# Eighteen weight differences of a decoder layer, on GpSimd in place of VectorE

## The chip, the cores and the metric

The kernel runs on one core of a Trainium2 chip. The time is device time in microseconds (us) of one execution, the median of the runs. A core has four engines that compute here: TensorE (PE in the profile) multiplies matrices, VectorE (DVE) and ScalarE (ACT) work elementwise, and GpSimd (POOL) is a fourth, programmable engine that this kernel uses mainly to issue some DMAs. SyncE (SP) issues most of the other DMAs. Each engine works through its own queue in order; engines wait for each other and for DMAs through semaphores.

## The reference

One decoder layer on 256 tokens of width 2048, in float32. Cut to what matters:

```
h    = rms_norm(x, pre_norm_w)
proj = h @ w_in                         # all projections and gates at once
oa   = gated_delta_rule(conv(q), conv(k), conv(v), beta, g)   # branch A, 8 heads
u_a  = (norm(oa) * silu(z_a)) @ w_branch_a        # 1024 -> 2048
ob   = block_attention(q, k, v) * silu(z_b)       # branch B, 8 heads
u_b  = ob @ w_branch_b                            # 1024 -> 2048
y    = (sigmoid(ga) * u_a + sigmoid(gb) * u_b) @ w_out        # 2048 -> 2048
out  = x + rms_norm(y, post_norm_w)
```

## The kernel before

Every large product is made from halves: a float32 tile is cast to a shorter form (`hi`, on ACT, line 218) and the rest is taken as a second tile (`lo = raw - hi`, on DVE, line 219), and TensorE multiplies hi by hi, hi by lo and lo by hi. Weights stream from HBM in blocks of 128 x 4 x 512 numbers (1 MB); each block is split in two sets of 128 x 1024. The pool that holds the `hi` and `lo` tiles has three buffers of each, so ACT and DVE can be up to three sets ahead of TensorE. Both inputs of the `lo` subtraction lie in SBUF.

Some of the matrix products are replaced by a scheme of the Strassen kind: a product of 2 x 2 blocks is made with seven block products in place of eight (`seven`). It needs four sums of the left side's blocks and four of the weight's. The weight's quarters that enter the sums are loaded unsplit (`fetch`, line 726, DMAs issued by GpSimd) into three tiles `tq[0]`, `tq[1]`, `tq[2]`; `differences` (lines 728 to 735) then forms, in place, `tq[0] - tq[2]`, `tq[1] - tq[0]` and `tq[1] - tq[2]`, each in two instructions of 128 x 1024 numbers: six a group. A fourth difference is formed later by DVE inside `seven` (line 786). The three groups are the two column pairs of `w_branch_a` (products named `ua0p` and `ua2p`) and one part of `w_out` (`yp`). In the profile the first group's tiles are called `tq_g` and `tq_z`, those of the others `tq`. All the groups reuse buffers: the second and third lie in the same three (`z0`, `z1`, `z2`), one of which the first uses as well, so a group is fetched as tiles of the one before come free.

The first product that reads a difference is `p5`, the second of the seven; `p6` and `p7` follow. As in any other product, each difference is split by ACT and DVE before TensorE multiplies with it.

What sets the order: TensorE's instructions keep the order in which the program traces them (`pin`, that is `keep_in_program_order`, which ties an instruction behind the one traced before it on its engine). Side work sits in queues of generators (`Queue`); after every few matmuls `tick()` advances them, and a `yield` of some number waits that many ticks' worth. The differences are one such generator, in queue `sq`, which waits `T_WAIT` (5, 7, 7) and then hands out one instruction per unit. The six are pinned on DVE in the kernel before. What is not pinned, such as the splits and the DMAs, is put in order on its engine by the planner that builds the program, by when it takes the inputs to be ready.

Beside the differences of the first group runs the end of the attention branch (scores of a head at lines 1010 to 1016, the keys' scaling at line 1055) and the projections `ga`, beside the second the gate `gb` (`raw_gb`, `lo_gb`), beside the third the last of `gb` and the projection `ub`.

Of the kernel before, what the change touches and what calls it, by code (L numbers as in the profile page):

```python
# [12 lines left out]
ALU = mybir.AluOpType  # L13
# [61 lines left out]
def hybrid_layer(  # L75
# [15 lines left out]
    nc = tc.nc  # L91
# [49 lines left out]
    pin = tc.keep_in_program_order  # L141
# [586 lines left out]
    def differences(tq, c, wait):  # L728
        yield wait
        for o, a, b in ((0, 0, 2), (1, 1, 0), (2, 1, 2)):  # L730
            for u in range(2):
                us = slice(2 * u, 2 * u + 2)
                pin(nc.vector.tensor_tensor(tq[o][:, us], tq[a][:, us], tq[b][:, us], op=ALU.subtract))
                yield 1
        formed.append(c)

# [97 lines left out]
    def next_differences(w, c):  # L834


        for q in aq + bq:
            q.drain()
        tqs.append([big.tile([P, 4, 512], F32, tag=f"z{i}", name=f"tq{len(tqs)}_{i}") for i in range(3)])
        for i in (2, 0, 1) if len(tqs) == 2 else (1, 0, 2):  # L840
            fetch(tqs[-1], w, c, i)
        formed.clear()
        sq.add(differences(tqs[-1], c, T_WAIT[len(tqs) - 1]))

    def solve():
# [136 lines left out]
        for i in (0, 2, 1):  # L982
            fetch(tqs[0], wa, 0, i)
        sq.add(differences(tqs[0], 0, T_WAIT[0]))
        yield OS_WAIT
        while attended[0] < H:
# [290 lines left out]
```

## Time and profile before

| | |
|---|---|
| median of 3 runs | 782.95 us (782.21 to 784.22) |
| the profiled execution | 782.22 us |
| its span, first to last instruction | 780.4 us |
| mean granted TensorE clock | 0.998 |
| differences on DVE | 18, from 439.1 to 645.0 us |

A row of a timeline reads: start, duration (us), engine, line, operation, output <- inputs by the program's names, shapes, count, and in brackets how long the engine was idle before it and what ended that. A row of waits reads: who waited for whom, us in total, times, the longest. A row of a grouped view gives the count, then busy time and the mean ns of one. PEld is TensorE's loading of weights, which lies beside its multiplications. Busy TensorE is not TensorE at its peak; spans on POOL are rough.

### The profile page before, as it was taken

Reading aid. Unit: us, or ns where it says so; the run is one execution under the profiler, and the core shown is the slowest. Engines: PE = TensorE matmul, PEld = TensorE weight load, DVE = VectorE, ACT = ScalarE, POOL = GpSimd, SP = SyncE. Lnnn points to the kernel's source line nnn. Section 1 sums busy time; section 2 is a strip of 40 time slices with the busy share of each in tenths; the row PEclk is TensorE's granted clock in tenths of the full one; section 3 lists DMA queues with packets and bytes.
Section 4 is the critical chain, followed back from the end, with each engine's and each line's share of the span. In section 5 each row is a group of like instructions: output and inputs, shape, how many; then the busy total and the mean of one; then the engine's idle time right before and its main releaser. Section 6 shows DMA issues by size and latency. Waiting matters only on the chain.

```text
span 780.4 us, 10345 instructions
## 1 busy us (share of the span) xinstructions
PE 765.1 (98%) x3923; PEld 651.2 (83%) x3923; DVE 564.1 (72%) x914; ACT 424.7 (54%) x642; POOL 31.5 (4%) x57
## 2 busy tenths in 40 slices
PE   8999999998999999999999999999999999999996
PEld 7898988897888888888888888878887788887884
DVE  5777669885867899775546785685748677878753
ACT  5676665655545544554447574654456544556641
POOL 3000001111000000002001000000000000000000
PEclk9999999999999999999999999999999999999999
DMA  8576675468865657659434557557563965475822
GB/s 300 173 235 214 188 211 169 135 185 205 244 207 167 211 165 214 174 161 244 123 109 166 212 165 249 206 202 247 176 212 129 356 215 169 155 259 187 312 106 108
DMA packets 93656, 153.44 MB, mean 197 GB/s; under 512 B 3237, under 2 KB 46886, under 8 KB 92966
## 3 DMA queue, kind: packets, MB, share of 16 engines
q1 hardware_dynamic: 88902, 134.42, 53.4%
q0 software_dynamic: 3936, 15.21, 5.5%
q10 hardware_dynamic: 768, 3.15, 1.6%
q8 instruction: 31, 0.51, 0.3%
q14 instruction: 19, 0.16, 0.1%
HBM read 149.61 MB, written 3.15 MB: 196 GB/s over the span
## 4 chain that ended last, share of the span: by engine, by line
PE 91%; DVE 3%; ACT 3%; DMA 2%; issue 1%; SPq 0%; DVEq 0%; ACTq 0%
PE a_gb L144 11%; PE a_ga L144 11%; PE a_y L144 10%; PE a_zg L144 6%; PE a_mk L144 6%; PE a_k L144 6%; PE a_ub L144 6%; PE a_zm L144 6%; PE a_mq L144 5%; PE a_mv L144 5%; PE a_v L144 5%; PE a_q L144 4%; PE a_ua L144 3%; PE sv L144 2%; PE s L144 1%
## 5 line engine op out<-in xcount | busy, mean ns | idle before, releaser
L144 PE MATMUL a_ga<-hi_ga,hT 128*128 128x512 f32 x256 | 82.2, 393 | 0.0
L144 PE MATMUL a_gb<-hi_gb,hT 128*128 128x512 f32 x256 | 79.9, 390 | 0.0
L219 DVE TENSOR_TENSOR lo_gb<-raw_gb,hi_gb 128x1024 fp32r<-128x1024 f32 x32 | 38.7, 1224 | 25.9 <-ACT hi_gb L218 25.7
L144 PEld LDWEIGHTS a_gb<-hi_gb,hT 128*128 128x128 f32 x256 | 48.1, 188 | 10.0
L144 PEld LDWEIGHTS a_ga<-hi_ga,hT 128*128 128x128 f32 x256 | 48.1, 188 | 9.8
L219 DVE TENSOR_TENSOR lo_ga<-raw_ga,hi_ga 128x1024 fp32r<-128x1024 f32 x32 | 38.8, 1221 | 17.9 <-ACT hi_ga L218 17.8
L144 PE MATMUL a_gb<-lo_gb,hT 128*128 128x512 f32 x128 | 50.4, 394 | 0.6 <-DVE lo_gb L219 0.4
L144 PE MATMUL a_ga<-lo_ga,hT 128*128 128x512 f32 x128 | 50.1, 391 | 0.7 <-DVE lo_ga L219 0.7
L218 ACT CAST hi_gb<-raw_gb 128x1024 fp32r<-128x1024 f32 x32 | 33.3, 1052 | 31.9 <-PE a_gb L144 24.4
L218 ACT CAST hi_ga<-raw_ga 128x1024 fp32r<-128x1024 f32 x32 | 33.5, 1052 | 30.9 <-PE a_ga L144 16.7
L144 PE MATMUL a_zg<-hi_zg,hT 128*128 128x348 f32 (+1 forms) x192 | 47.0, 322 | 0.0
L144 PE MATMUL a_v<-hT,hi_v 128*128 128x512 f32 x128 | 45.4, 398 | 1.4 <-ACT hi_v L218 1.4
L144 PE MATMUL a_mq<-hT,hi_mq 128*128 128x512 f32 x128 | 46.7, 405 | 0.0
L144 PE MATMUL a_mk<-hT,hi_mk 128*128 128x512 f32 x128 | 46.0, 401 | 0.0
L144 PE MATMUL a_y<-hi_y,mT 128*128 128x512 f32 x144 | 45.9, 391 | 0.0
L144 PE MATMUL a_q<-hT,hi_q 128*128 128x512 f32 x128 | 45.8, 398 | 0.0
L144 PE MATMUL a_ub<-hi_ub,obT 128*128 128x512 f32 x128 | 41.0, 393 | 0.0
L144 PE MATMUL a_k<-hT,hi_k 128*128 128x512 f32 x128 | 40.6, 400 | 0.0
L144 PE MATMUL a_zm<-hi_zm,hT 128*128 128x512 f32 x128 | 40.6, 392 | 0.0
L144 PE MATMUL a_mv<-hi_mv,hT 128*128 128x512 f32 x128 | 40.1, 391 | 0.0
L144 PE MATMUL a_v<-hT,lo_v 128*128 128x256 f32 x128 | 36.1, 282 | 1.4 <-DVE lo_v L219 1.4
L144 PE MATMUL a_q<-hT,lo_q 128*128 128x256 f32 x128 | 35.9, 280 | 0.0
(375 smaller groups left out, 1962.4 us busy)
## 6 DMA issues: line engine op xcount, KB each, us to landing
raw_ga<-in_w_in_dram SPq DMA_DIRECT2D x16, 1024.0 KB, 5.3
raw_gb<-in_w_in_dram SPq DMA_DIRECT2D x16, 1024.0 KB, 5.2
raw_y<-in_w_out_dram SPq DMA_DIRECT2D x15, 1024.0 KB, 5.3
raw_q<-in_w_in_dram SPq DMA_DIRECT2D x8, 1024.0 KB, 5.7
raw_mv<-in_w_in_dram SPq DMA_DIRECT2D x8, 1024.0 KB, 5.0
raw_v<-in_w_in_dram SPq DMA_DIRECT2D x8, 1024.0 KB, 10.7
raw_zm<-in_w_in_dram SPq DMA_DIRECT2D x8, 1024.0 KB, 5.1
raw_mq<-in_w_in_dram SPq DMA_DIRECT2D x8, 1024.0 KB, 5.9
```

The costliest lines, as they stand in the source:

```text
L144: return pin(nc.tensor.matmul(*args, **kwargs))
L218: nc.scalar.copy(hi, raw)
L219: nc.vector.tensor_tensor(lo, raw, hi.bitcast(F32), op=ALU.subtract)
```

## The change

The six subtractions of each group are issued on GpSimd in place of VectorE, and without `pin`. The tiles, the ticks and the fetches stay as they are, and so does the fourth difference in `seven`.

```
@@ differences(tq, c, wait) @@
         for o, a, b in ((0, 0, 2), (1, 1, 0), (2, 1, 2)):
             for u in range(2):
                 us = slice(2 * u, 2 * u + 2)
-                pin(nc.vector.tensor_tensor(tq[o][:, us], tq[a][:, us], tq[b][:, us], op=ALU.subtract))
+                nc.gpsimd.tensor_tensor(tq[o][:, us], tq[a][:, us], tq[b][:, us], op=ALU.subtract)
                 yield 1
```

More of the change, by code (lines that the diff above doesn't have):

```diff
@@ L732, in differences @@
                 us = slice(2 * u, 2 * u + 2)
-                pin(nc.vector.tensor_tensor(tq[o][:, us], tq[a][:, us], tq[b][:, us], op=ALU.subtract))
+                nc.gpsimd.tensor_tensor(tq[o][:, us], tq[a][:, us], tq[b][:, us], op=ALU.subtract)
                 yield 1
```

## The prediction

> **What bounds the kernel now.** I read the page first, then the list of TensorE's waits, then the three stretches in which the 18 differences run, and in those the order of single instructions. The profiled execution took 782.22 us, 780.4 of it the span; the median of the three timed runs, 782.95, is 0.7 above it, so 0.7 is added to a sum at the end. A change under 0.3% of it (2.35 us) counts as none: the runs themselves lie 2.0 us apart.
>
> ```profile
> span 780.4 us, 10345 instructions
> PE 765.1 (98%) x3923; PEld 651.2 (83%) x3923; DVE 564.1 (72%) x914; ACT 424.7 (54%) x642; POOL 31.5 (4%) x57
> PE 91%; DVE 3%; ACT 3%; DMA 2%; issue 1%; SPq 0%; DVEq 0%; ACTq 0%
> ```
>
> TensorE (PE) is busy 98% of the span and 91% of the chain that ended last. VectorE (DVE) has 72%, GpSimd (POOL) 4%. So time goes only where PE is made to wait, and what is to be asked of a change on DVE and POOL is whether PE waits more or less. The waits of PE on DVE behind the first differences, and on the outputs just ahead of them:
>
> ```profile
> PE a_ga L144 <- DVE lo_ga L219: 0.7, 2, 0.4
> PE pt L147 <- DVE oz L913: 0.5, 1, 0.5
> PE a_gb L144 <- DVE lo_gb L219: 0.4, 1, 0.4
> PE a_y L144 <- DVE lo_y L219: 0.4, 1, 0.4
> ```
>
> They make 2.0 us. In the stretches that hold the differences (stretch, length, busy time of PE, PEld, DVE, ACT and POOL, granted clock, DMA) there are none:
>
> ```profile
> 436.00:464.00 28.00, 28.00 (x145) 23.66 (x144) 24.67 (x37) 18.10 (x31) 0.00 (x0) 1.00 0.50 169
> 536.00:566.00 30.00, 30.00 (x134) 24.86 (x133) 20.28 (x18) 12.86 (x13) 0.00 (x0) 1.00 0.61 205
> 625.00:650.00 25.00, 25.00 (x112) 20.71 (x111) 18.27 (x16) 10.75 (x11) 0.00 (x0) 1.00 0.60 207
> ```
>
> PE is busy in all of 28, 30 and 25 us at a clock of 1.00, and POOL does nothing.
>
> **What is removed.** Six differences for each of the three groups:
>
> ```profile
> L733 DVE TENSOR_TENSOR tq<-tq,tq x12: 1217/1218/1220, 545.1 to 645.0; 128x1024 f32<-128x1024 f32 x12
> L733 DVE TENSOR_TENSOR tq_g<-tq_g x2: 1216/1216/1217, 439.1 to 443.0; 128x1024 f32<-128x1024 f32 x2
> L733 DVE TENSOR_TENSOR tq_z<-tq_z,tq_g x2: 1207/1212/1217, 446.5 to 448.9; 128x1024 f32<-128x1024 f32 x2
> L733 DVE TENSOR_TENSOR tq_g<-tq_z,tq_g x2: 1215/1216/1216, 456.6 to 460.3; 128x1024 f32<-128x1024 f32 x2
> ```
>
> 18 x 1.22 = 21.9 us of DVE time go. PE waits for DVE nowhere in these stretches, so this is worth nothing to the end: a gain of 0.
>
> **When POOL starts.** On POOL a difference waits only for its quarters to land and for POOL's own queue; the ticks at which it is handed out no longer delay it, and nothing keeps it in place. POOL's rows (issue of the loads), and issue to landing of four of them:
>
> ```profile
> 421.50 1.53 POOL L726 DMA_DIRECT2D tq_g<-in_w_branch_a_dram  x2 [61.08 <-ACT jo L898]
> 427.52 0.75 POOL L726 DMA_DIRECT2D tq_z<-in_w_branch_a_dram  x1 [4.50 <-DVE oz L913]
> 528.84 0.75 POOL L726 DMA_DIRECT2D tq<-in_w_branch_a_dram  x1 [36.23 <-DVE lo_ua0p L219]
> 615.01 0.75 POOL L726 DMA_DIRECT2D tq<-in_w_out_dram  x1 [11.33 <-DVE lo_ua2p L219]
> ```
> ```profile
> tq_g<-in_w_branch_a_dram POOLq DMA_DIRECT2D x1, 1024.0 KB, 8.4
> tq_z<-in_w_branch_a_dram POOLq DMA_DIRECT2D x1, 1024.0 KB, 8.9
> tq<-in_w_branch_a_dram POOLq DMA_DIRECT2D x1, 1024.0 KB, 5.6
> tq<-in_w_out_dram POOLq DMA_DIRECT2D x1, 1024.0 KB, 6.4
> ```
>
> The second load of the first row was issued at 421.50 + 0.77 = 422.3 and landed 8.4 later. So the first two differences can start at 430.7, the next four at 427.52 + 8.9 = 436.4; the second group's six at 528.84 + 5.6 = 534.4, the third's at 615.01 + 6.4 = 621.4. No load of POOL is queued behind a group but the next group's, which needs the same buffers empty, and the two at the end of the kernel, at 695.8 and later: moving the differences into POOL's queue delays no transfer.
>
> **When they must be done.** The first ACT cast that reads a group, per group:
>
> ```profile
> 508.62 1.05 ACT L218 CAST hi_ua0p<-tq_g 128x1024 fp32r<-128x1024 f32 x1 [1.67 <-PE a_ga L144]
> L218 ACT CAST hi_ua2p<-tq x8: 1048/1055/1057, 578.3 to 612.4; 128x1024 fp32r<-128x1024 f32 x8
> L218 ACT CAST hi_yp<-tq x8: 1047/1055/1057, 694.7 to 725.2; 128x1024 fp32r<-128x1024 f32 x8
> ```
>
> (For the first group this is its third set, formed last.) From 436.4 to 508.6, 534.4 to 578.3 and 621.4 to 694.7 there are 72, 44 and 73 us. The cover runs out only where one POOL difference takes over 18 us in the first group (four of them after 436.4) or 22 in the second (the two that its first product reads). As a latency the change costs 0.
>
> **What a POOL difference takes.** No row shows this form on POOL. The nearest rows of POOL:
>
> ```profile
> L623 POOL TENSOR_SCALAR_AFFINE_SELECT tv<-tv 32x1024 f32<-32x1024 f32 x4 | 4.6, 1141 | 0.3
> L621 POOL MEMSET tv<- 128x1024 f32 x1 | 0.9, 942 | 0.0
> ```
>
> One input of the same length in and out takes 1.14 us, writing alone 0.94. With all streams side by side a difference takes 1.14; with its two inputs one behind the other 2.28; with the write behind both 3.22. I take the middle, since the select's 1.14, which holds a read and a write, is near the 0.94 of the write alone, so that the write hides and only the second read adds. The Trainium skill (GPSIMD Engine Reference, Performance versus the Vector engine) gives 4.497 us for twice this length, an estimate of 2.25, by which the sum below would be 0.5 lower; no row here shows it.
>
> **What it does to DVE.** This is the unknown that decides. Six differences back to back are some 14 us in which POOL reads and writes SBUF while DVE goes on making `lo` halves out of two SBUF tiles. The trace has no moment at which both do so, so the cost is bounded: at 0, if they run side by side, and, if one holds the other up for the length of an instruction, by the following count. The rows of the second group:
>
> ```profile
> 535.82 1.23 DVE L219 TENSOR_TENSOR lo_gb<-raw_gb,hi_gb 128x1024 fp32r<-128x1024 f32 x1 [1.12 <-ACT hi_gb L218]
> 538.54 1.22 DVE L219 TENSOR_TENSOR lo_gb<-raw_gb,hi_gb 128x1024 fp32r<-128x1024 f32 x1 [1.49 <-ACT hi_gb L218]
> ```
> ```profile
> 537.46 1.05 ACT L218 CAST hi_gb<-raw_gb 128x1024 fp32r<-128x1024 f32 x1 [1.67 <-PE a_gb L144]
> ```
> ```profile
> 542.92 0.39 PE L144 MATMUL a_gb<-lo_gb,hT 128*128 128x512 f32 x1
> ```
>
> A `lo` every 2.72 us. There are three buffers, and the cast of 537.46 waited for PE to free one, so PE is two sets of 2.72 us away from the `lo` that ends at 538.54 + 1.22 = 539.76: its first use is the row at 542.92, a slack of 3.15 us. If POOL and DVE take turns, one turn is 2.28 + 1.22 = 3.50, and each `lo` falls 0.78 further behind its 2.72. DVE had been idle 1.12 before the row of 535.82, so it is free at 534.7 and lets POOL in; POOL holds until 537.0, the next `lo` ends at 538.2 instead of 537.05, late by 1.17. With five more turns the sixth is late by 1.17 + 5 x 0.78 = 5.1, and PE stands 5.1 - 3.15 = **1.9 us**. The third group has the same beat, with POOL in at 621.4:
>
> ```profile
> 621.98 1.22 DVE L219 TENSOR_TENSOR lo_gb<-raw_gb,hi_gb 128x1024 fp32r<-128x1024 f32 x1 [1.10 <-ACT hi_gb L218]
> ```
>
> First lateness 621.4 + 2.28 - 621.98 = 1.7, the sixth 5.6, less 3.15: **2.5 us**. In the first group other work stands in DVE's queue:
>
> ```profile
> 440.24 0.42 DVE L1055 TENSOR_TENSOR y_mk<-y_mk,rrow 128x256 f32<-128x256 f32 x1
> 447.73 1.21 DVE L219 TENSOR_TENSOR lo_ga<-raw_ga,hi_ga 128x1024 fp32r<-128x1024 f32 x1
> ```
> ```profile
> 449.42 0.39 PE L144 MATMUL a_ga<-lo_ga,hT 128*128 128x512 f32 x1
> ```
>
> From 430.7, six differences (13.7), the four `lo` between them (4.9) and two multiplies of the key rows like this one (0.8) end at 450.1. The `lo` of 447.73 is then done at 451.3 where PE wants it at 449.42: **1.9 us**. What is queued behind a held `lo` is all of DVE's work; here the attention's maxima and reciprocals, which fit beside POOL's last two.
>
> The sum by turns is 1.9 + 2.5 + 1.9 = 6.3 us: 782.2 + 6.3 = 788.5 as profiled, **789.2** as a median. With 1.14 for a difference a turn is 2.36, under 2.72, and nothing is lost; at 2.05 the same count gives 2.1 us, just inside what counts as none. With 3.22 a turn is 4.44: 1.72 per `lo`, so 2.1 + 8.6 - 3.15 = 7.6, 2.6 + 8.6 - 3.15 = 8.1, and 1.9 + 6 x 0.94 = 7.5 us, 23.2 in all, 806.1. I take turns over side by side as a judgement: no row speaks against either, but there is no row from which a gain could come.
>
> The Trainium skill (SBUF — State Buffer, Who interferes with whom, and the section on SBUF's two sides) says that GpSimd's one port pair is VectorE's second one, held exclusively for a whole instruction against a VectorE instruction with two SBUF inputs. By it the turns hold, and the sum is 789.2; without it, 783. No run so far shows it.
>
> **The rivals.**
> - *Side by side.* POOL's reads leave DVE's `lo` at 1.22 us, or stretch it to no more than 2.72, which the beat hides. For it: DVE is idle 1.49 before the `lo` of 538.54. Against it: nothing measured. Time 783.0, within 0.3%. Chance 0.24.
> - *POOL keeps its place* for all six. Then a `lo` asked for at 535.8 ends at 534.7 + 13.7 + 1.2 = 549.6, late by 12.6, and PE stands 9.4 per group: some 28 us, 811. For it: POOL's next difference is always ready. Against it: DVE's `lo` is waiting at each change. Chance 0.07.
> - *Faster.* In the first stretch DVE is busy 24.67 of 28 us and has the `lo` of 447.73 only 0.5 us ahead of its use; without the differences it runs up to 3.7 us earlier. It would decide if this took away PE's waits on DVE; those are 2.0 us in all, none in the stretch, so even all of them give 780.9, and a faster kernel needs order changes elsewhere too. Chance 0.05.
> - *The differences come late*, or POOL's unpinned order puts a load behind them. PE would stand at the second product of a group. It takes 18 us per difference: 0.02, with over 800.
>
> **How the numbers follow.** Turns have the remaining 0.62, of which 0.10 lies at differences so short (under 2.05 us) that less than 2.35 us is lost. Their own range is 784 to 800. Side by side has too much to leave out, so the range starts at 781.8 and ends at 800, leaving POOL's holding on, the 3.22 end and the faster case outside. Slower: 0.52 + 0.07 + 0.02, and 0.02 of side by side with a `lo` stretched past its beat = 0.63. Within: 0.10 + 0.22 = 0.32. Faster 0.05.
>
> **What would show it.** Right: `lo` rows of about 2 to 3.5 us (or as long a gap before them) at 431 to 450, 535 to 556 and 622 to 643, and PE waits on `lo` there of 1 to 3 us each, while the 18 POOL rows end long before 508, 578 and 694. Wrong: `lo` at 1.22 throughout and PE still busy all through these stretches; or POOL rows far from 2.3 us, which move the sum by the count above; or a difference on POOL that PE waits for.

## The result

The changed kernel takes 793.0 us (median; 792.45 to 794.31) against 783.5 for the kernel before on the same chip: 1.0125 times as long, 95% interval 1.0111 to 1.0140, or 9.5 us more. The forecast was slower, 789.2 us, in a range of 781.8 to 800. The changed kernel's profiled execution took 794.31 us, 12.1 more than that of before; 1.7 of these lie ahead of the first difference, where nothing was changed, and are scatter between two executions.

The page of the changed kernel, the lines that answer to those shown of before:

```profile
span 792.5 us, 10357 instructions
PE 770.6 (97%) x3923; PEld 654.8 (83%) x3923; DVE 572.9 (72%) x896; ACT 424.6 (54%) x642; POOL 88.4 (11%) x75
PE 86%; DVE 8%; ACT 3%; issue 1%; DMA 1%; SPq 0%; DVEq 0%; ACTq 0%
```

DVE lost 18 instructions of 1.22 us and yet is busy 572.9 us in place of 564.1. Its share of the chain that ended last rose from 3 to 8%. The differences on POOL (count, then shortest, median and longest ns), and the splits beside the second group in the kernel before and in the changed one:

```profile
L733 POOL TENSOR_TENSOR tq<-tq,tq x12: 2790/3384/3396, 546.5 to 644.2; 128x1024 f32<-128x1024 f32 x12
L733 POOL TENSOR_TENSOR tq_g<-tq_g x2: 2393/2887/3381, 432.4 to 434.7; 128x1024 f32<-128x1024 f32 x2
```
```profile
L219 DVE TENSOR_TENSOR lo_gb<-raw_gb,hi_gb x9: 1220/1225/1227, 535.8 to 557.7; 128x1024 fp32r<-128x1024 f32 x9
```
```profile
L219 DVE TENSOR_TENSOR lo_gb<-raw_gb,hi_gb x8: 1212/2788/3426, 545.8 to 567.1; 128x1024 fp32r<-128x1024 f32 x8
```

A split goes from 1.22 to as much as 3.43 us, and a difference takes 2.39 when it runs first and 3.38 once the two alternate: each row holds the engine's own time and the wait for the other. Singly, one split of the second group, and the six differences beside it:

```profile
557.03 3.42 DVE L219 TENSOR_TENSOR lo_gb<-raw_gb,hi_gb 128x1024 fp32r<-128x1024 f32 x1
```
```profile
546.55 19.52 POOL L733 TENSOR_TENSOR tq<-tq,tq 128x1024 f32<-128x1024 f32 x6 [6.93 <-DMA tq<-in_w_branch_a_dram]
```

3.42 - 1.22 = 2.2 us is what one difference holds a split up. The waits of PE that are new (the first) or grown (the second, from 0.4):

```profile
PE ms L144 <- DVE y_mk L1055: 5.7, 2, 4.8
PE a_gb L144 <- DVE lo_gb L219: 2.1, 4, 1.1
```

All 3923 matmuls come in the same order in both traces, so the n-th is the same matmul in both and tells where the time went in. The slip (start after less start before) grows at three places, the three groups:

| place | start before | start after | slip | grown by |
|---|---|---|---|---|
| last product ahead of the first group's scores `ms` | 442.2 | 443.9 | 1.7 | scatter |
| transposes `pp`, behind the first group | 451.9 | 462.0 | 10.1 | 8.4 |
| `a_ua`, behind the second group's | 575.3 | 586.1 | 10.8 | 0.7 |
| `a_ub`, behind the third group's | 639.7 | 651.8 | 12.1 | 1.3 |
| end of the span | 780.4 | 792.5 | 12.1 | 0 |

The three groups make 10.4 us; the medians differ by 9.5, and the runs of the kernel before lie 2.0 apart. Most of it is one place. VectorE's and TensorE's rows there:

```profile
442.93 2.16 DVE L1055 TENSOR_TENSOR y_mk<-y_mk,rrow 128x256 f32<-128x256 f32 x1
445.02 3.36 DVE L219 TENSOR_TENSOR lo_ga<-raw_ga,hi_ga 128x1024 fp32r<-128x1024 f32 x1
448.97 1.89 DVE L1055 TENSOR_TENSOR y_mk<-y_mk,rrow 128x256 f32<-128x256 f32 x1
```
```profile
450.92 1.65 PE L144 MATMUL ms<-y_mk,y_mq 128*128 128x128 f32 x4 [4.85 <-DVE y_mk L1055]
453.22 1.05 PE L144 MATMUL a_ga<-hi_ga,hT 128*128 128x512 f32 x2
```

The scaling of the second head's keys (line 1055) takes 0.42 us undisturbed. It has two SBUF inputs as a split has, is held up itself (1.89), and stands behind a held split (3.36) and a held first scaling (2.16). TensorE's order is fixed, the scores `ms` come next in it, and TensorE stands 4.85 us although products of `ga` behind `ms` have their data. Matmul by matmul, the 8.4 us of this place are 1.0 in front of the first head's scores, 5.1 in front of the second's, and 2.3 more from there to the eleventh product of `ga` behind them, which came 2.96 us after these scores before (443.06 to 446.02) and comes 5.21 after them now (450.92 to 456.13); the two products of the last row take 1.05 us where such a pair took 0.62. The granted clock says why:

```profile
445.00:452.00 7.00, 2.00 (x8) 1.51 (x9) 7.00 (x10) 1.64 (x2) 5.59 (x2) 0.76 0.29 111
452.00:456.00 4.00, 4.00 (x12) 3.14 (x11) 2.90 (x9) 1.98 (x8) 0.00 (x0) 0.56 0.00 0
456.00:464.00 8.00, 8.00 (x40) 6.66 (x39) 3.14 (x3) 3.87 (x5) 0.00 (x0) 1.00 0.53 155
```

0.56 for the 4 us that begin 1.1 us behind the gap, then 1.00. In finer windows of the same trace the clock is 0.84 from 448 to 449 us, 0.50 from 449 to 455 and 0.74 from 455 to 456: it fell some 2.6 us into the gap, at about 448.7, and stayed at half until about 455.5, for the first 4.6 us of work. Half of 4.6 us is the 2.3 us.

The Trainium skill (TensorE: Matmul & The Clock Gate, Part 1) has the clock at half after an idle window of about 3.4 us, and at full again after about 3.4 us of sustained work. The trace agrees on the half; on the idle time it differs, since the fall came 2.6 us into the gap, and shorter gaps were followed by one too (last section).

### The profile page after: what moved, and what is told of

It reads as the page before. It is cut to its first block, busy times and chain, and to the rows that moved or that the text cites. A ratio compares the mean times of both kernels' runs of the same rounds, so it can differ in the third digit from the quotient of the medians.

```text
span 792.5 us, 10357 instructions
## 1 busy us (share of the span) xinstructions
PE 770.6 (97%) x3923; PEld 654.8 (83%) x3923; DVE 572.9 (72%) x896; ACT 424.6 (54%) x642; POOL 88.4 (11%) x75
## 4 chain that ended last, share of the span: by engine, by line
PE 86%; DVE 8%; ACT 3%; issue 1%; DMA 1%; SPq 0%; DVEq 0%; ACTq 0%
PE a_y L144 10%; PE a_ga L144 10%; PE a_gb L144 8%; PE a_v L144 6%; PE a_k L144 6%; PE a_zg L144 6%; PE a_ub L144 6%; PE a_zm L144 6%; PE a_mq L144 5%; PE a_mv L144 5%; PE a_mk L144 5%; PE a_q L144 4%; PE a_ua L144 3%; DVE lo_gb L219 2%; PE sv L144 2%
## 5 line engine op out<-in xcount | busy, mean ns | idle before, releaser
L219 DVE TENSOR_TENSOR lo_gb<-raw_gb,hi_gb 128x1024 fp32r<-128x1024 f32 x32 | 55.6, 1765 | 20.3 <-ACT hi_gb L218 20.2
L219 DVE TENSOR_TENSOR lo_ga<-raw_ga,hi_ga 128x1024 fp32r<-128x1024 f32 x32 | 44.4, 1395 | 22.4 <-ACT hi_ga L218 22.3
L144 PEld LDWEIGHTS a_ga<-hi_ga,hT 128*128 128x128 f32 x256 | 48.9, 191 | 10.1
L733 POOL TENSOR_TENSOR tq<-tq,tq 128x1024 f32<-128x1024 f32 x12 | 38.9, 3276 | 19.8 <-DMA tq<-in_w_out_dram 12.9
## 6 DMA issues: line engine op xcount, KB each, us to landing
raw_v<-in_w_in_dram SPq DMA_DIRECT2D x8, 1024.0 KB, 10.8
```

The source lines that it names most:

```text
L144: return pin(nc.tensor.matmul(*args, **kwargs))
L219: nc.vector.tensor_tensor(lo, raw, hi.bitcast(F32), op=ALU.subtract)
L733: nc.gpsimd.tensor_tensor(tq[o][:, us], tq[a][:, us], tq[b][:, us], op=ALU.subtract)
```

## The experiments

Times are medians beside the kernel before, run on the same chip: 782.64 us for the first four, 782.75 for the last four. Diffs are against the changed kernel.

**One group, or the other two.**

```
-                nc.gpsimd.tensor_tensor(tq[o][:, us], tq[a][:, us], tq[b][:, us], op=ALU.subtract)
+                if tq is tqs[0]:              # e1; in e2: is not
+                    nc.gpsimd.tensor_tensor(tq[o][:, us], tq[a][:, us], tq[b][:, us], op=ALU.subtract)
+                else:
+                    pin(nc.vector.tensor_tensor(tq[o][:, us], tq[a][:, us], tq[b][:, us], op=ALU.subtract))
```

> Only the first group's six differences are on GpSimd; the other twelve are pinned on VectorE as before. Turns (GpSimd and VectorE's two-SBUF-input instructions shut each other out for a whole instruction): in the changed kernel the matmul sequence slips by 8.4 us around the first group, nearly all of it where the scores ms wait for the second key scaling, so 783.5 + 8 = 791.5 us here. Rival, order: the loss comes of VectorE's and GpSimd's instructions being handed out in another order over the whole kernel; then no part holds most of it, some 786 to 788. Rival, sharing: VectorE is only slowed in proportion; it says nothing on which group, but the long holds of a scaling of 0.42 us (2.16 and 1.89 in the changed kernel) speak against it.

> Only the second and third groups' twelve differences are on GpSimd. Turns: the slips of 0.7 and 1.3 us seen around these groups, so 783.5 + 2 = 785.5 us. Order: the other half of the loss, 787 or more.

The first group alone: 791.29 us, ratio 1.0100 (1.0082 to 1.0119), 8.7 us more. The other two alone: 784.86 us, 1.0032 (1.0021 to 1.0044), 2.2 more. The new waits of PE are those of the changed kernel, one to each:

```profile
PE ms L144 <- DVE y_mk L1058: 5.8, 2, 4.8
```
```profile
PE a_gb L144 <- DVE lo_gb L219: 2.4, 5, 1.1
```

(Line 1058 here is 1055 of the changed kernel.) The loss is local to where the differences run, and the place weighs more than the amount: six differences cost four times what the other twelve do. The rival of an order changed over the whole kernel, which had 786 to 788 us for the first run, is out.

**No differences at all.** This kernel leaves out all 18, on either engine; its products go by the loaded quarters.

```
             for u in range(2):
                 us = slice(2 * u, 2 * u + 2)
-                nc.gpsimd.tensor_tensor(tq[o][:, us], tq[a][:, us], tq[b][:, us], op=ALU.subtract)
                 yield 1
```

> The 18 differences are left out (their tiles keep the loaded quarters), on either engine: what taking 21.9 us from VectorE is worth with nothing put in its place. By the prediction nothing, since TensorE waits for VectorE nowhere beside the differences: 783.5 us, within 1. Rival, relief: VectorE's freed time shortens waits elsewhere, 781 or less. Order: a loss without any GpSimd work, 785 or more.

782.69 us, ratio 0.9994 (0.9983 to 1.0005). VectorE's 21.9 us are worth nothing that can be measured. The first stretch of it, where VectorE was busy 24.67 us of 28 before:

```profile
436.00:464.00 28.00, 28.00 (x146) 23.65 (x145) 19.14 (x32) 17.99 (x32) 0.00 (x0) 1.00 0.53 175
```

19.14 now, and TensorE busy all the 28 us in both. So another engine that takes over the differences can gain no more on this kernel than the interval leaves, some 0.2%; it can only keep from losing.

**Shorter and longer GpSimd instructions.**

```
 # e4: halves
-                us = slice(2 * u, 2 * u + 2)
-                nc.gpsimd.tensor_tensor(tq[o][:, us], tq[a][:, us], tq[b][:, us], op=ALU.subtract)
+                for k in (2 * u, 2 * u + 1):
+                    nc.gpsimd.tensor_tensor(tq[o][:, k], tq[a][:, k], tq[b][:, k], op=ALU.subtract)
 # e5: wholes
-            for u in range(2):
-                us = slice(2 * u, 2 * u + 2)
-                nc.gpsimd.tensor_tensor(tq[o][:, us], tq[a][:, us], tq[b][:, us], op=ALU.subtract)
-                yield 1
+            nc.gpsimd.tensor_tensor(tq[o], tq[a], tq[b], op=ALU.subtract)
+            yield 2
```

> Each GpSimd difference is made in two instructions of 128 x 512, 36 in all; the amount of work is the same. Turns: a hold lasts about 1.1 us in place of 2.2, a turn 1.1 + 1.14 = 2.25 us, below the beat of 2.72, so the second and third groups lose 0 to 0.5 each, and in the first each VectorE instruction is held half as long, 1 to 3 us: 785 to 787 us. Sharing in proportion: the amount read is the same, so 793 us as in the changed kernel.

> Each difference is one GpSimd instruction of 128 x 2048, nine in all; the amount of work is the same. Turns: a hold of about 4.4 us, a turn 4.4 + 1.14 = 5.5 us, in which the beat of 2.72 wants two splits: each of the three turns of the second group costs 2.8, the first up to 4.4, so 8 to 10 less the 3.15 of slack, 5 to 7 us; the third group the same; the first about as in the changed kernel, since three holds of 4.4 last as long as six of 2.2. In all 799 to 806 us. Sharing in proportion: 793 us.

Halves: 784.2 us, ratio 1.0021 (1.0008 to 1.0035). Wholes: 803.8 us, 1.0267 (1.0242 to 1.0293). The splits beside the second group, halves and then wholes:

```profile
L219 DVE TENSOR_TENSOR lo_gb<-raw_gb,hi_gb x9: 1214/1856/2340, 536.9 to 558.8; 128x1024 fp32r<-128x1024 f32 x9
```
```profile
L219 DVE TENSOR_TENSOR lo_gb<-raw_gb,hi_gb x6: 1210/2882/5598, 543.2 to 562.2; 128x1024 fp32r<-128x1024 f32 x6
```

The longest split is 2.34, 3.43 and 5.60 us for differences of 512, 1024 and 2048 numbers a partition: 1.1, 2.2 and 4.4 above 1.22, one GpSimd instruction each time. The same 18 x 1024 numbers a partition are subtracted in all three kernels, and the loss goes from 1.6 over 9.5 to 21 us. Sharing in proportion to what is read would give one time for all; a hold for the length of an instruction gives these three. With halves a turn (2.27 us by the median row of POOL) stays below the beat of 2.72 us, so no lateness piles up, and the loss of 1.6 us is inside the 1.5 to 3.5 above 783.5 that were expected. With wholes the second and third group cost 6.0 and 5.9 us of slip, inside the 5 to 7 expected, but not by holds alone: behind a gap of TensorE of 2.50 us in the one and 2.39 in the other the clock was 0.50 for some 3.4 us, about 1.7 us of each that the expectation didn't count. Without it the holds come to some 4.3 and 4.2, less than expected.

The Trainium skill (SBUF — State Buffer, the section on SBUF's two sides) has whichever of the two engines starts first keep the port pair that they share for the whole instruction while the other fully blocks; the holds of 1.1, 2.2 and 4.4 us agree. The Trainium skill (GPSIMD Engine Reference, Performance versus the Vector engine) has 4.497 us for a GpSimd addition of 2048 numbers; the first whole difference took 4.60 here, and the prediction's estimate from that figure, 2.25 us, is near the 2.2 held.

**GpSimd that only writes.**

```
-        for o, a, b in ((0, 0, 2), (1, 1, 0), (2, 1, 2)):
+        for o in (0, 1, 2):
             for u in range(2):
-                us = slice(2 * u, 2 * u + 2)
-                nc.gpsimd.tensor_tensor(tq[o][:, us], tq[a][:, us], tq[b][:, us], op=ALU.subtract)
+                nc.gpsimd.memset(tq[o], 0.0)
```

> In place of the 18 differences GpSimd writes zeros over the whole tile they would have written (18 memsets of 128 x 2048, 1.9 us each by the row of 0.942 us for half of it): GpSimd busy as long as before, but without reading SBUF. The differences are left out. If what shuts the engines out is GpSimd's reading: splits stay at 1.22 us beside the memsets and the time is 783.5 us. If any GpSimd instruction on SBUF does: holds of 1.9 us, turns of 3.0, 788 to 791 us.

783.18 us, ratio 1.0008 (0.9997 to 1.0019): no change. The memsets of the two later groups, and the splits in a window with two of them (they began at 533.78):

```profile
L732 POOL MEMSET tq<- 128x2048 f32 x12 | 21.8, 1813 | 26.4 <-DMA tq<-in_w_branch_a_dram 16.7 <-DMA tq<-in_w_out_dram 9.4
```
```profile
535.22 1.23 DVE L219 TENSOR_TENSOR lo_gb<-raw_gb,hi_gb 128x1024 fp32r<-128x1024 f32 x1 [1.10 <-ACT hi_gb L218]
```

A split that starts beside a 1.8 us memset still takes 1.23. The memsets wait for one tile each, so some ran ahead of the crowded stretches; still, 16 splits of this trace overlap a memset, and all take 1.21 to 1.23, and a key scaling that does takes 0.43. So a GpSimd that is busy writing doesn't hold VectorE up, and one that subtracts does; what a subtraction does beyond a memset is to read SBUF. A GpSimd instruction that reads one input only was not tried.

**The key scaling with one input from PSUM**, alone and with halves.

```
-        kTs = [halves(pk[m], f"mk{h + m}") for m in range(2)]
-        for m in range(2):
-            nc.vector.tensor_tensor(kTs[m], kTs[m], rrow, op=ALU.mult)
+        kTs = []
+        for m in range(2):
+            y = wk.tile([P, S], F32, tag="f256", bufs=8, name=f"y_mk{h + m}")
+            nc.scalar.copy(y, pk[m][:, S:])
+            nc.vector.tensor_tensor(pk[m][:, :S], pk[m][:, :S], y, op=ALU.add)
+            nc.vector.tensor_tensor(y, pk[m][:, :S], rrow, op=ALU.mult)
+            kTs.append(y)
```

> The changed kernel, but the four-quarter sum of the keys is left in its PSUM bank and scaled from there, so that this one multiplication (line 1055) has one SBUF input and one PSUM input in place of two SBUF inputs. Turns: it is no longer held; the first wait of ms (0.87) goes, and the second scaling comes about 3.7 us earlier, at the end of the split ahead of it, so PE's wait for it falls from 4.85 to about 1, and with it the stretch of matmuls at the lower clock: 787 to 789 us. If VectorE is held whatever its inputs are: 793 us.

> Halved GpSimd instructions and the key scaling from PSUM together. Turns: what is left is the splits' lateness in the first group, 783.5 to 785.5 us. It also shows whether the differences on GpSimd can be had for nothing; none of the reasons gives less than the kernel before.

Alone: 787.02 us, ratio 1.0055 (1.0040 to 1.0070): 4.3 above the kernel before, where the changed one was 9.5 above its own. All eight scalings, their own row and what waits for them:

```profile
L1058 DVE TENSOR_TENSOR y_mk<-a_mk,rrow x8: 408/424/426, 341.2 to 444.8; 128x256 f32<-128x256 f32 x8
```
```profile
PE ms L144 <- DVE y_mk L1058: 1.8, 1, 1.8
```
```profile
431.00:464.00 33.00, 31.24 (x169) 26.43 (x168) 28.01 (x36) 18.05 (x30) 17.40 (x6) 1.00 0.56 187
```

No scaling is held any more, beside the same six GpSimd differences: VectorE is held only where both inputs are in SBUF. What is left here is 1.8 us of wait behind a held split in VectorE's queue, and the clock stays at 1.00. The first group's slip falls from 8.4 to 2.0 us; the later groups still cost 1.2 and 1.1. With halves as well: 783.42 us, ratio 1.0017 (1.0007 to 1.0028), 0.7 us above the kernel before. No version was faster than the kernel before, as the run without differences had already bounded.

## Why the prediction was right, and where it was off

*The change is worth no time on VectorE*: right. Leaving the differences out moves nothing.

*Turns, not side by side*: right, and with it the sign. The choice, called a judgement then, is now settled by the three lengths of instruction and by the memsets.

*2.28 us for a difference*: right in size, 2.2 held. A turn, taken as 3.50, was 3.38 by the median row of POOL.

*1.9 and 2.5 us for the second and third group*: too high, 0.7 and 1.3 of slip. The turn was shorter, so that a `lo` fell some 0.66 behind its beat in place of 0.78; and the second group's last load, issued at 538.87, landed 7.5 us later, not 5.6, so that the first turn met a split in another phase and made it 0.6 late, not 1.17.

*1.9 us for the first group*: this is the term that was mis-sized; it was 8.4, 6.1 of it waits and 2.3 the clock behind them. The step that failed is the use that I took for the first to be late. I counted four `lo` and the two multiplies of the key rows into the lateness of the `lo` of 447.73, and let PE stand only there. But PE wants the second scaling earlier, for `ms`, in a fixed order, and that scaling is itself one of the held instructions. In the trace it comes behind five of POOL's six and waits for the sixth. So the largest wait, 4.85 us, was on a scaling, where the prediction's signs named waits on `lo` of 1 to 3 us. A sum of holds has to be set against every instruction of the stretch that TensorE waits for, not the one with the thinnest slack in the quiet trace. The scaling from PSUM took 6.4 us of this back. Second, the clock fell in the gap of 4.85 us, and cost 2.3 us which no term held. That the total came within 3.8 us is in part luck: the first group was under-counted by 6.5 and the later ones over-counted by 2.4.

*Moving the differences into POOL's queue delays no transfer*: wrong, though the lateness itself cost nothing. In the third group the planner put the first two differences ahead of the third load, which then had to wait for them:

```profile
622.52 6.48 POOL L733 TENSOR_TENSOR tq<-tq,tq 128x1024 f32<-128x1024 f32 x2 [7.97 <-DMA tq<-in_w_out_dram]
628.94 0.76 POOL L726 DMA_DIRECT2D tq<-in_w_out_dram  x1
```

Before it was issued at 615.0, with the slip until then 626 to 627: so 2 to 3 us late, against 70 us of cover. The same order put two differences at a place where TensorE had no slack:

```profile
630.13 0.50 PE L144 MATMUL a_gb<-lo_gb,hT 128*128 128x512 f32 x1 [1.09 <-DVE lo_gb L219]
```

That wait is nearly all of the third group's 1.3 us; it is not the piling up that was counted, which, with four differences left and a later start, stayed inside the slack.

*The differences are done in time*: right; nothing waited for a difference. POOL's keeping its place for all six didn't happen: splits and differences alternate one by one.

## What to carry to other kernels

Work moved to an idle GpSimd isn't off VectorE's path where it reads SBUF: here each of its subtractions, once begun, kept a VectorE instruction with two SBUF inputs waiting to its end (1.1, 2.2 or 4.4 us at most), while VectorE instructions with a PSUM input were not held, and GpSimd's pure writes held nothing. Count the hold against every instruction in VectorE's queue that TensorE, in its fixed order, will want in that stretch, and keep hold plus instruction below the beat: halving the GpSimd instructions took back 8 of 9.5 us. And first ask whether the time to be freed is worth anything: leaving the work out was the one run that answered that, and the answer was no.

## What the runs showed that was not expected

A gap of TensorE of 4.85 us cost nearly half more than its length, since the clock was at 0.50 for the first 4.6 us of work behind it. Which gaps do this can't be read off their length alone. One of 1.8 us (the scaling from PSUM) left the clock at 1.00; two of 2.50 and 2.39 us (whole differences) were each followed by 0.50 for some 3.4 us. And far ahead of the differences, at about 195 us, both the kernel before and the changed one have waits of 1.41 and 0.81 us close together: in the profiled execution of the first the clock shows 1.00 from 194 to 199 us, in that of the second 0.66 from 195 to 200. That stretch is some 0.6 of the 1.7 us of scatter.

A GpSimd row's duration tells little of the engine's own work: the same subtraction shows 2.39 us at its first and 3.38 in alternation with VectorE, the rest being the wait.
